# A decoder step on one core: other numbers for the planner of the recorded order, the two plain gate columns ahead of the two up columns, and the last residual block summed and squared in its bank

## The chip, the cores and the metric

One NeuronCore of a Trainium2 chip. The metric is the time of one execution on the device in microseconds, the median over the runs. The engines are TensorE (PE; its weight loads are shown apart as PEld), VectorE (DVE), ScalarE (ACT), GpSimd (POOL) and SyncE (SP), which issues most DMAs. Matmuls write to PSUM, eight banks of 128 x 512 fp32; everything else works in SBUF.

## The reference

One layer of a decoder for 512 prompt tokens and 8 x 4 sample tokens (544 columns in all), width 1024, fp32:

```
z = rmsnorm(x, norm_mix) @ w_in         # split: attention q, k, v; HGRN q, f, i, g
att = dilated_attention(q, k, v)        # 8 heads, three (window, dilation) patterns
f = lb + (1 - lb) * sigmoid(f);  o, s = hgrn2_recurrence(silu(q), 1 - f, i, log f)   # 4 heads
x = x + concat([head_rmsnorm(att), head_rmsnorm(o) * silu(g)]) @ w_out
x = x + cross_attention(rmsnorm(x, norm_cross), memory) @ w_co
u = rmsnorm(x, norm_ffn)
x = x + (silu(causal_conv3(u @ w_gate)) * (u @ w_up)) @ w_down      # 2816 columns
y = rmsnorm(x, norm_final)
```

The new keys and values, the HGRN states and the last gate rows are outputs too.

## The kernel before

All activations lie transposed in SBUF: x is eight tiles x[0] to x[7] of 128 features by 544 tokens. A product in fp32 accuracy is three fp32r matmuls (high by high, high by low, low by high part); weights are loaded (wr), cast to the high part by ACT (wh) and subtracted to the low part by DVE (wl). A token row is done in two cuts of 256 and 288 columns.

**The recorded order.** The kernel's code doesn't issue instructions. Every call goes to a `Tape` (line 240 on), which records it as a `Step` with its engine, length and dependences; at the end `run()` puts all steps in an order by a list scheduling on a model of the five engines, and issues them. All instructions so come from one line, L638 (DMAs L612). A product that is recorded under `main()` is a *main* step of PE; mains keep their recorded order. Other PE steps (scores, transposes, HGRN products) are *side* steps. When PE is free, the next main goes, unless side steps that are ready amount to `BURST` us, or the first of them has waited longer than `PATIENCE`, or one is due: then a burst of sides goes. A step's due time (`begin`) is reckoned back from its users (`due()`), with `MARGIN` us to spare ahead of a main; the other engines take steps up to `LEAD` us ahead of their due time, the earliest due first. The five numbers stand in line 259.

**The stages.** From 0 to about 320 us: the columns of w_in one after the other as mains (ps_z_q, ps_z_v and the like), among them as sides the dilated attention (psd, psS, psT, psO, psdo) and the four HGRN heads. A head's recurrence is done by levels: DVE makes the factors kq for windows of 1, 2, 4 and up to 64 tokens, PE multiplies them (psB for the smallest, psA, psL for the largest); ACT copies psA to hsm, POOL masks that to hvm, DVE adds up htm and hAT; psu, psU, hS carry the state; psin goes through DVE's hin and back through the same bank, and pso is the head's output. In the last head, memory products (ps_ck, ps_cv) are the mains. Then W_out, the cross-attention, and from 438 us the feed-forward.

**The feed-forward.** 22 column blocks of w_gate and w_up. The first `PLAIN` = 2 are plain products (`plain_tile`, line 2043; ps_g, ps_u in two cuts each). A gate column's bank is read out as ug by DVE (`weighed`), and goes through the convolution (ACT, then two DVE passes), silu (ACT) and a product with the row norm on DVE (cv); an up column's bank is read by the product with that (`up`). The other twenty go in pairs by a Strassen scheme of seven products (`Pair`; ps_ag, ps_dg, ps_cg and, for up, ps_au and so on), whose weight sums S1 to S4 and the part whg, wlg come from two weight columns; the sums S1g and S3g are made by a DMA that adds, issued by POOL. The first pair's first product (ps_ag with whg, wlg) stands ahead of the second half of the last plain column (`seq.insert(-1, ...)`, line 2270). The eight down blocks go in between, ps_d.

**The end.** The last four column blocks of w_down (`DOWN_LAST`) make eight blocks m in two cuts c, ps_dz, in three banks taken in turn (`PF`). For each, `last_half` (line 2317) adds the bank to x[m] (`add_to`, on DVE), squares the sum on ACT and adds that to ssq3's accumulator acc_final (on POOL, for m = 6 on DVE); for m = 7 the square stays apart as sq_last. `final(c)` (line 2336) sums over partitions by two matmuls (psr_final, on acc_final and on sq_last), makes 1/sqrt by Ln and two Exp on ACT (r_final in PSUM, r_fin in SBUF), multiplies into y and issues the output DMAs.

Of the kernel before, what the change touches and what calls it, by code (L numbers as in the profile page):

```python
# [250 lines left out]
class Tape:  # L251
# [4 lines left out]

    BURST, PATIENCE, SLACK, LEAD, MARGIN = 1.33, 3.05, 12.0, 12.06, 3.77


    BLOCK, FIRST, WAITS, FETCH = 256, 195, 1.0086, 6.0
# [380 lines left out]
def tile_decoder_step(ctx: ExitStack, tc: tile.TileContext, xT, memT, kwT, vw, s0, conv_in, mkT, mv, vecs, cst,  # L643
# [27 lines left out]
    def PF(name):  # L671

        turn[0] += 1
        return PDEC(name) if turn[0] % 3 == 0 else PD(name)
# [18 lines left out]
    def V(name, i=0):  # L693
        return vec[:, VEC_COLS[name][0] + i:VEC_COLS[name][0] + i + 1]
# [15 lines left out]
    resident |= {*range(len(specs), len(specs) + 12)}  # L710
    specs += [w_cq[i] for i in range(4)] + [w_co[i] for i in range(8)]
    ffn_w = len(specs)
    for j in range(PLAIN):
        specs += [w_gate[j], w_up[j]]

    class Weights:
        def __init__(self):
# [104 lines left out]
    stream = Stream()  # L822


    def passes(ps, w, xs, n0, n, order, first=True, last=True):
        for at, i in enumerate(order):
            (hi, lo), (xh, xl) = w[i], xs[i]
            for j, (a, b) in enumerate(((hi, xh), (hi, xl), (lo, xh))):
                nc.tensor.matmul(ps[:, :n], a, b[:, n0:n0 + n], start=(first and at == 0 and j == 0),
                                 stop=(last and at == len(order) - 1 and j == 2))  # L830

    def half(w, xs, name, evac, cut, order=None):
        n0, n = cut
# [1417 lines left out]

    gates, hids = {}, {}
    for q in range(2 * PLAIN):
        kind, j = "gu"[q % 2], q // 2
        done = plain_tile(kind, j, ffn_w + q, gates.get(j))
        if kind == "g":
            gates[j] = conv(j, done)
        else:
            hids[j] = gated(j, done)
# [46 lines left out]

    r_fin, last_sq = A("r_fin"), A("sq_last")
    hs, k = [hid[j] for j in range(*DOWN_LAST)], DOWN_LAST[1] - DOWN_LAST[0]
    ys = {}
    ON_POOL = (1, 3, 6), (1, 5)  # L2310

    def y_at(m, c):
# [4 lines left out]
    def last_half(m, c):  # L2317
        n0, n = LAST_CUTS[c]
        cut = slice(n0, n0 + n)
        if m == 0 and c == 1:  # L2320
            tape.gate_at = len(tape.mains) - 1
            nc.sync.dma_start(conv_out, last2)
            nc.scalar.preload_act_table_set(LN_SET)
            tape.gate_at = None
        ps = PF(f"ps_dz{m}_{c}")
        with tape.main():
            passes(ps, held[m], hs, n0, n, range(k))
        add_to(m)(ps, n0, n)
        if m < KT - 1:
            ssq3.add(x[m][:, cut], n0, nc.vector if m == KT - 2 else None)  # L2330
        else:
            nc.scalar.activation(last_sq[:, cut], x[m][:, cut], AF.Square)
        if m in ON_POOL[c]:
            nc.scalar.activation(y_at(m, c), x[m][:, cut], AF.Copy, scale=V("norm_final", m))

    def final(c):
        n0, n = LAST_CUTS[c]
        cut = slice(n0, n0 + n)
        ps = PX(f"psr_final{c}")
        for i, sq in enumerate((ssq3.acc, last_sq)):  # L2340
            nc.tensor.matmul(ps[:, :n], C("ones"), sq[:, cut], start=i == 0, stop=i == 1)
        nc.scalar.activation(r_fin[:, cut], ps[:, :n], AF.Ln, bias=eps, scale=1.0 / D)

        r = PX(f"r_final{c}")[:, :n]
        nc.scalar.activation(r, r_fin[:, cut], AF.Exp, scale=-0.5)
        nc.scalar.activation(r_fin[:, cut], r_fin[:, cut], AF.Exp, scale=-0.5)
        for m in range(KT):
            out = y_at(m, c)
            if m in ON_POOL[c]:
                nc.gpsimd.tensor_tensor(out, out, r_fin[:, cut], op=ALU.mult)  # L2350
            else:
                nc.vector.scalar_tensor_tensor(out, x[m][:, cut], V("norm_final", m), r, op0=ALU.mult, op1=ALU.mult)
            (nc.scalar if c and m % 2 else nc.sync).dma_start(yT[128 * m:128 * m + 128, cut], out)

    held = []
# [91 lines left out]
```

## Time and profile before

| | us |
|---|---|
| median of 3 runs | 820.3 (819.9, 820.3, 821.14) |
| the profiled run | 820.65 |
| its span | 818.8 |
| PE busy | 805.1 |
| DVE busy | 656.9 |
| ACT busy | 423.6 |
| POOL busy | 108.6 |

The span is from the first to the last event of the profiled execution; 1.85 us of its time lie outside. The granted clock of PE is 0.997 of full speed. A row of the timeline has the start, the length, the engine, the source line, the operation, out<-in by the program's names with buffer numbers left out, shapes, and in brackets how long the engine stood idle before it and what it waited for. A row of the waits of PE has what waited, for whom, the total, how often, and the longest.

### The profile page before, as it was taken

What the parts mean: (1) busy time and instruction counts of PE and PEld (TensorE: products, weight loads), DVE (VectorE), ACT (ScalarE), POOL (GpSimd) and SP (SyncE); (2) the same over time, 40 slices, a digit from 0 to 9 for tenths busy, and PEclk for the clock granted to TensorE, in tenths of its full rate; (3) what the DMA queues carried; (4) which work ended last, traced back from release to release, by engine and by line L of the source; (5) the groups of instructions that cost most, each with busy time, mean ns of one, the idle gap of its engine ahead of it and who ended that gap; (6) DMA issues with size and microseconds to landing.
All of it is one profiled execution on the core that took longest, in us unless ns stands there. A gap on an engine that the chain in (4) does not pass through costs nothing.

```text
span 818.8 us, 18897 instructions
## 1 busy us (share of the span) xinstructions
PE 805.1 (98%) x7515; PEld 755.4 (92%) x7515; DVE 656.9 (80%) x1486; ACT 423.6 (52%) x844; POOL 108.6 (13%) x187
## 2 busy tenths in 40 slices
PE   9999999999999999999999999999999999999996
PEld 9999986797889889998899999999999999999995
DVE  6997789987997997563679899987887788887854
ACT  7644364456557546444547655544554454445443
POOL 0040100010010000002201221222113012210113
PEclk9999999999999999999999999999999999999998
DMA  9439996956833544262522764556455565564503
GB/s 332 146 111 299 345 346 209 306 198 205 291 108 94 185 132 158 71 220 83 193 87 81 165 158 128 153 130 166 118 146 139 133 164 142 128 177 109 150 3 110
DMA packets 93064, 135.47 MB, mean 165 GB/s; under 512 B 6320, under 2 KB 60336, under 8 KB 92976
## 3 DMA queue, kind: packets, MB, share of 16 engines
q1 hardware_dynamic: 86208, 122.79, 46.5%
q0 software_dynamic: 5760, 10.49, 8.3%
q8 instruction: 59, 0.97, 0.5%
q10 hardware_dynamic: 1008, 0.99, 0.4%
q14 instruction: 29, 0.24, 0.1%
HBM read 126.17 MB, written 8.07 MB: 164 GB/s over the span
## 4 chain that ended last, share of the span: by engine, by line
PE 85%; DVE 9%; ACT 2%; DMA 2%; issue 1%; POOL 0%; SPq 0%; DVEq 0%
PE ps_d L638 13%; PE ps_ag L638 7%; PE ps_au L638 7%; PE ps_wo L638 6%; PE ps_cu L638 4%; PE ps_cg L638 4%; PE ps_co L638 3%; PE ps_dz L638 3%; PE ps_cq L638 3%; PE ps_z_v L638 2%; PE ps_du L638 2%; PE ps_dg L638 2%; DVE wl L638 2%; PE ps_z_Q L638 2%; PE ps_z_f L638 2%; PE ps_z_i L638 2%
## 5 line engine op out<-in xcount | busy, mean ns | idle before, releaser
L638 ACT CAST wh<-wr 128x1024 fp32r<-128x1024 f32 (+1 forms) x54 | 46.1, 871 | 57.0 <-issue 10.5
L638 DVE TENSOR_TENSOR wl<-wr,wh 128x1024 fp32r<-128x1024 f32 (+1 forms) x54 | 53.7, 1003 | 6.5 <-ACT wh L638 4.1
L638 DVE TENSOR_TENSOR xr<-xr,ps_d 128x256 f32<-128x256 f32 x80 | 34.7, 434 | 13.0 <-PE ps_d L638 12.6
L638 POOL COPY last<-ug 128x2 f32<-128x2 f32 (+1 forms) x44 | 22.1, 546 | 131.3 <-DVE ug L638 131.3
L638 DVE SCALAR_TENSOR_TENSOR cv<-ug,vec,cv 128x560 f32<-128x560 f32 x44 | 35.2, 800 | 1.0 <-ACT cv L638 0.2
L638 ACT ACTIVATE cv<-ug,vec 128x560 f32<-128x560 f32 x22 | 18.8, 857 | 27.9 <-DVE ug L638 27.9
L638 POOL TENSOR_TENSOR hvm<-hsm,cs 64x512 f32<-64x512 f32 x4 | 4.5, 1120 | 177.1 <-ACT hsm L638 132.6
L638 DVE TENSOR_TENSOR cv<-cv,r_ux 128x512 f32<-128x512 f32 (+1 forms) x44 | 18.9, 438 | 6.0 <-ACT cv L638 5.9
L612 POOL DMA_DIRECT2D S1u<-in_w_up x10 | 8.6, 861 | 100.4 <-DVE up L638 39.5
L638 POOL TENSOR_SCALAR cp<-cp,cden 128x256 f32<-128x256 f32 x8 | 7.9, 990 | 88.9 <-DVE cden L638 80.4
L638 ACT ACTIVATE P<-P,mx 128x128 f32<-128x128 f32 (+3 forms) x32 | 17.6, 552 | 3.7 <-DVE mx L638 3.7
L638 PE MATMUL ps_co<-coh,wh 128*128 128x256 f32 (+1 forms) x64 | 18.7, 292 | 0.0
L638 PE MATMUL ps_co<-coh,wl 128*128 128x256 f32 (+1 forms) x64 | 18.5, 289 | 0.0
L638 PE MATMUL ps_co<-col,wh 128*128 128x256 f32 (+1 forms) x64 | 18.4, 288 | 0.0
L638 ACT COPY keptg<-ps_ag 128x272 f32<-128x272 f32 x20 | 7.7, 383 | 20.1 <-PE ps_ag L638 20.1
L638 DVE TENSOR_TENSOR xr<-xr,ps_dz 128x288 f32<-128x288 f32 (+1 forms) x16 | 7.0, 438 | 13.3 <-PE ps_dz L638 13.3
L638 ACT COPY keptu<-ps_au 128x272 f32<-128x272 f32 x20 | 7.7, 385 | 19.1 <-PE ps_au L638 19.1
L638 DVE TENSOR_TENSOR keptg<-ps_cg,keptg 128x272 f32<-128x272 f32 x20 | 8.8, 440 | 10.8 <-PE ps_cg L638 10.4
L638 DVE TENSOR_TENSOR xr<-xr,ps_wo 128x256 f32<-128x256 f32 (+1 forms) x16 | 6.8, 437 | 12.5 <-PE ps_wo L638 12.5
L638 POOL COPY ug<-conv_state 128x16 f32<-128x16 f32 x22 | 14.8, 670 | 14.0 <-DMA conv_state<-in_conv_in 6.2
L638 DVE TENSOR_TENSOR keptu<-ps_cu,keptu 128x272 f32<-128x272 f32 x20 | 8.8, 438 | 9.7 <-PE ps_cu L638 9.7
L638 ACT ACTIVATE cv<-cv 128x560 f32<-128x560 f32 x22 | 14.8, 675 | 2.6 <-DVE cv L638 2.6
(3773 smaller groups left out, 3680.0 us busy)
## 6 DMA issues: line engine op xcount, KB each, us to landing
st<-in_kwT SPq DMA_DIRECT2D x32, 448.0 KB, 6.2
st<-in_vw SPq DMA_DIRECT2D x28, 512.0 KB, 6.1
wd<-in_w_down SPq DMA_DIRECT2D x32, 256.0 KB, 3.2
wr<-in_w_in SPq DMA_DIRECT2D x15, 512.0 KB, 6.9
wrg<-in_w_gate SPq DMA_DIRECT2D x10, 512.0 KB, 5.6
wru<-in_w_up SPq DMA_DIRECT2D x10, 512.0 KB, 5.5
st<-in_mkT SPq DMA_DIRECT2D x8, 512.0 KB, 4.8
wr<-in_w_out SPq DMA_DIRECT2D x8, 512.0 KB, 3.7
```

The lines of the kernel that those rows point to most:

```text
L612: return tape.put(engine, lambda: call(*args, **kw), outs, ins, 0.1, 0.3, size)
L638: return tape.put(engine, lambda: call(*args, **kw), outs, ins, length, lag, size, port, words)
```

## The change

It has three parts. The first sets other numbers in line 259 and so the order of the steps of the whole program. The second turns the order of the plain columns' weights and products from g0, u0, g1, u1 to g0, g1, u0, u1. The third concerns block m = 7 of the second cut: ACT copies x[7] into the bank ahead of the products, these accumulate on it without a start flag, ACT squares the bank directly, and the last product for y reads the bank, with the norm from SBUF (r_fin). The sum of the squares of m = 5 in this cut moves from POOL to DVE. The matmuls are the same in number and shape.

```diff
--- before.py
+++ after.py
@@ -256,7 +256,7 @@
 
 
 
-    BURST, PATIENCE, SLACK, LEAD, MARGIN = 1.33, 3.05, 12.0, 12.06, 3.77
+    BURST, PATIENCE, SLACK, LEAD, MARGIN = 0.77, 3.65, 12.0, 16.11, 3.44
 
 
     BLOCK, FIRST, WAITS, FETCH = 256, 195, 1.0086, 6.0
@@ -710,8 +710,7 @@
     resident |= {*range(len(specs), len(specs) + 12)}
     specs += [w_cq[i] for i in range(4)] + [w_co[i] for i in range(8)]
     ffn_w = len(specs)
-    for j in range(PLAIN):
-        specs += [w_gate[j], w_up[j]]
+    specs += [w_gate[j] for j in range(PLAIN)] + [w_up[j] for j in range(PLAIN)]
 
     class Weights:
         def __init__(self):
@@ -822,12 +821,12 @@
     stream = Stream()
 
 
-    def passes(ps, w, xs, n0, n, order, first=True, last=True):
+    def passes(ps, w, xs, n0, n, order, first=True, last=True, loose=False):
         for at, i in enumerate(order):
             (hi, lo), (xh, xl) = w[i], xs[i]
             for j, (a, b) in enumerate(((hi, xh), (hi, xl), (lo, xh))):
                 nc.tensor.matmul(ps[:, :n], a, b[:, n0:n0 + n], start=(first and at == 0 and j == 0),
-                                 stop=(last and at == len(order) - 1 and j == 2))
+                                 stop=(last and at == len(order) - 1 and j == 2), skip_group_check=loose)
 
     def half(w, xs, name, evac, cut, order=None):
         n0, n = cut
@@ -2251,7 +2250,7 @@
 
     gates, hids = {}, {}
     for q in range(2 * PLAIN):
-        kind, j = "gu"[q % 2], q // 2
+        kind, j = "gu"[q // PLAIN], q % PLAIN
         done = plain_tile(kind, j, ffn_w + q, gates.get(j))
         if kind == "g":
             gates[j] = conv(j, done)
@@ -2306,7 +2305,7 @@
 
     r_fin, last_sq = A("r_fin"), A("sq_last")
     hs, k = [hid[j] for j in range(*DOWN_LAST)], DOWN_LAST[1] - DOWN_LAST[0]
-    ys = {}
+    ys, last = {}, []
     ON_POOL = (1, 3, 6), (1, 5)
 
     def y_at(m, c):
@@ -2323,11 +2322,20 @@
             nc.scalar.preload_act_table_set(LN_SET)
             tape.gate_at = None
         ps = PF(f"ps_dz{m}_{c}")
+        whole = m == KT - 1 and c == 1
+        if whole:
+            tape.gate_at = len(tape.mains) - 1
+            nc.scalar.copy(ps[:, :n], x[m][:, cut])
+            tape.gate_at = None
         with tape.main():
-            passes(ps, held[m], hs, n0, n, range(k))
+            passes(ps, held[m], hs, n0, n, range(k), not whole, loose=whole)
+        if whole:
+            nc.scalar.activation(last_sq[:, cut], ps[:, :n], AF.Square)
+            last.append(ps[:, :n])
+            return
         add_to(m)(ps, n0, n)
         if m < KT - 1:
-            ssq3.add(x[m][:, cut], n0, nc.vector if m == KT - 2 else None)
+            ssq3.add(x[m][:, cut], n0, nc.vector if m >= KT - 2 - c else None)
         else:
             nc.scalar.activation(last_sq[:, cut], x[m][:, cut], AF.Square)
         if m in ON_POOL[c]:
@@ -2349,7 +2357,8 @@
             if m in ON_POOL[c]:
                 nc.gpsimd.tensor_tensor(out, out, r_fin[:, cut], op=ALU.mult)
             else:
-                nc.vector.scalar_tensor_tensor(out, x[m][:, cut], V("norm_final", m), r, op0=ALU.mult, op1=ALU.mult)
+                src, rows = (last[0], r_fin[:, cut]) if c and m == KT - 1 else (x[m][:, cut], r)
+                nc.vector.scalar_tensor_tensor(out, src, V("norm_final", m), rows, op0=ALU.mult, op1=ALU.mult)
             (nc.scalar if c and m % 2 else nc.sync).dma_start(yT[128 * m:128 * m + 128, cut], out)
 
     held = []
```

The order of the instructions changes most in the stages ahead of W_out. Two places there and one in the feed-forward:

PE in the first HGRN head (minus is before, plus is after; psd and psS are attention scores against the cache and the new keys, kq0_32 and kq0_64 the factors of the two largest windows, psA0 the middle windows):

```order
-L638 MATMUL psL0_196<-kq0_32_194 32x32 x8
+L638 MATMUL psS020_432<-z_k0_167,z_q0_223 128x384
+L638 MATMUL psS021_433<-z_k0_167,z_q0_223 128x384
+L638 MATMUL psd11_413<-st30_470,qbd_win_155 32x224 x4
 L638 MATMUL psA0_189<-kq0_8_188 32x32 x16
 L638 MATMUL psA0_189<-kq0_16_193 32x32 x16
 L638 MATMUL psA0_189<-cs_73,z_i0_175 32x128 x2
-L638 MATMUL psd11_413<-st29_469,qbd_win_155 32x224 x4
-L638 MATMUL psd11_413<-knew_156,qbd_win_155 32x32 x4
+L638 MATMUL psL0_196<-kq0_32_194 32x32 x8
 L638 MATMUL psL0_196<-kq0_64_197 64x64 x4
```

The scores psS02 come ahead of psA, and psL's first product goes behind psA.

PE in the last HGRN head (hsm, hin, hAT, hS are what DVE and ACT make of the products; ps_cv are the memory's value products):

```order
 L638 MATMUL psin3_806<-hst31_801,z_Q3_739 32x128 x4
+L638 MATMUL psu30_811<-hvm3_809,hsm3_794 128x512
+L638 MATMUL psu31_812<-hvm3_809,hsm3_794 128x512
+L638 MATMUL psin3_806<-hsm3_794 128x32
+L638 MATMUL psin3_806<-cs2_74,hin3_814 128x32 x2
+L638 MATMUL pso3_815<-hAT3_797,hvt3_807 128x128 x2
+L638 MATMUL pso3_815<-z_Q3_739,hS3_813 128x128
+L638 MATMUL pso3_815<-hAT3_797,hvt3_807 128x128
+L638 MATMUL pso3_815<-z_Q3_739,hS3_813 128x128
+L638 MATMUL pso3_815<-hAT3_797,hvt3_807 128x128
+L638 MATMUL pso3_815<-z_Q3_739,hS3_813 128x128
 L638 MATMUL ps_cv0_921<-wh19_924,mmh0_757 128x512
```

psu, psin's second use and pso now follow psin's first use at once; they stood among and behind the first six ps_cv products.

DVE in the plain columns, before (ug1 is the second gate column, S1g2 to S4g2 weight sums, wlg2 the low weight part of the first pair, cv1 the convolution):

```order
L638 TENSOR_TENSOR S1g2l_1263<-S1g2_1239,S1g2h_1262 128x512
L638 TENSOR_TENSOR h0l_1218<-up0_1214,h0h_1217 128x544
L638 TENSOR_TENSOR S2g2l_1242<-S2g2_1240,S2g2h_1241 128x512
L638 TENSOR_TENSOR S3g2l_1256<-S3g2_1254,S3g2h_1255 128x512
L638 TENSOR_TENSOR ug1_1221<-ps_g1_256_1223,r_ux_1129 128x256
L638 TENSOR_TENSOR ug1_1221<-ps_g1_256_1223,r_ux_1129 128x8x4
L638 TENSOR_TENSOR S4g2_1276<-S2g2_1240,wrg2_1230 128x512
L638 TENSOR_TENSOR wlg2_1232<-wrg2_1230,whg2_1231 128x1024
L638 SCALAR_TENSOR_TENSOR cv1_1224<-ug1_1221,vec_72,cv1_1224 128x560 x2
```

and after:

```order
L638 SCALAR_TENSOR_TENSOR cv1_1217<-ug1_1214,vec_72,cv1_1217 128x560 x2
L638 TENSOR_TENSOR up0_1220<-ps_u0_256_1222,cv0_1211 128x256
L638 TENSOR_TENSOR up0_1220<-ps_u0_256_1222,cv0_1211 128x32
L638 TENSOR_TENSOR S2g2_1240<-S1g2_1239,wrg2_1230 128x512
L638 TENSOR_TENSOR S3g2l_1256<-S3g2_1254,S3g2h_1255 128x512
L638 TENSOR_TENSOR wlg2_1232<-wrg2_1230,whg2_1231 128x1024
L638 TENSOR_TENSOR cv1_1217<-cv1_1217,r_ux_1129 128x512
L638 TENSOR_TENSOR up1_1228<-ps_u1_0_1229,cv1_1217 128x256
L638 TENSOR_TENSOR S2g2l_1242<-S2g2_1240,S2g2h_1241 128x512
```

wlg2 now follows S3g2l at once, and what concerned the second gate column is done before, save for cv1.

## The prediction

> **What bounds the kernel now.** I read the page first, then the waits of TensorE (PE), then the timeline at each of those waits, then sums by windows. The page:
>
> ```profile
> span 818.8 us, 18897 instructions
> PE 805.1 (98%) x7515; PEld 755.4 (92%) x7515; DVE 656.9 (80%) x1486; ACT 423.6 (52%) x844; POOL 108.6 (13%) x187
> ```
>
> PE works 805.1 of 818.8 us. The change leaves its matmuls as they are, so whatever it wins or loses is in the other 13.7 us, or in new waits. Where they lie, by the waits of PE (total, times, longest):
>
> ```profile
> PE psL L638 <- DVE kq L638: 1.5, 1, 1.5
> PE ps_g L638 <- DVE up L638: 1.3, 1, 1.3
> PE ps_first L638 <- DVE zero L638: 1.1, 1, 1.1
> PE psr_final L638 <- DVE acc_final L638: 0.8, 1, 0.8
> PE ps_z_q L638 <- DVE z_q L638: 0.5, 1, 0.5
> PE psA L638 <- DVE kq L638: 0.4, 1, 0.4
> PE psr_hg L638 <- DVE htm L638: 0.3, 1, 0.3
> PE ps_ag L638 <- DVE wlg L638: 0.2, 1, 0.2
> ```
>
> 6.1 us in eight waits; the rest, some 7.6 us, is nearly all the end, behind the last matmul. ps_first is the start and ps_z_q stands as it was; the other six lie in places that the new order rebuilds. That is the most there is to win by order, and a kernel so full can lose as easily: a wait that PE doesn't have today costs its whole length.
>
> **Part 1, the planner's numbers: head 1 of the HGRN part.** Here VectorE makes kq level by level and PE consumes it (psA, psL). Timeline rows (start, length, instruction):
>
> ```profile
> 121.37 0.56 PE L638 MATMUL psd<-st,qbd_win 128*32 128x224 f32 x8
> 121.48 0.42 DVE L638 TENSOR_TENSOR kq<-hq,hf 128x256 f32<-128x256 f32 x1
> 122.04 0.38 PE L638 MATMUL psL<-kq 128*32 128x32 f32 x13
> 123.27 0.26 ACT L638 COPY hsm<-psA 64x128 f32<-64x128 f32 x1 [0.17 <-PE psA L638]
> 123.61 1.14 POOL L638 TENSOR_TENSOR hvm<-hsm,cs 64x512 f32<-64x512 f32 x1 [18.88 <-ACT hsm L638]
> 123.77 1.26 DVE L638 TENSOR_TENSOR kq<-hq,hf 128x256 f32<-128x256 f32 x1
> 125.18 0.65 PE L638 MATMUL psL<-kq 128*64 128x64 f32 x8 [1.50 <-DVE kq L638]
> 129.29 0.92 PE L638 MATMUL psS<-z_k,z_q 64*128 64x384 f32 x4
> ```
>
> The last kq took 1.26 us where its like takes 0.42: it ran beside GpSimd's hvm. PE waited 1.50 for it. In the new order psS (0.9) and the psA products stand ahead of psL. PE got to this psL at 123.7 (125.18 less 1.50); with psS more and one psd and its companion less (0.5 by the first row) it gets there near 124.1. hsm and hvm move as well, by psS's 0.9 less the 0.35 of the smaller psL that stood ahead of psA and now stands behind it: hvm starts near 124.15. kq, on VectorE in its old place, starts at 123.77 and should end near 124.2. The 0.4 at psA goes too, with a psd product ahead of it. Gain 1.9 less a remainder of 0.1: **1.8** (0.6 if hvm is first again, 1.9 at best).
> On who is first, the Trainium skill says (SBUF — State Buffer, "SBUF: two separate sides") that VectorE with two SBUF inputs and GpSimd share a pair of ports as an exclusive lock, which whoever starts first keeps for its whole instruction. The row bears it out roughly: kq ended at 125.03, 0.28 after hvm. By it my 1.8 stands only while kq starts before hvm; by the rows alone I would have charged kq for the overlapped part and taken 1.5.
>
> The 0.3 at psr_hg, which now stands behind a whole product, goes (**0.3**); for new small waits in the same stretch, 135 to 205 us, I take **0.2** (0 to 0.7, the longest like it being psA's and psr_hg's together).
>
> **Part 1, heads 2 and 3.** There PE is full and VectorE nearly so. Windows: start and end, length, then busy time of PE, PEld, DVE, ACT, POOL. And the rows at both ends of the argument:
>
> ```profile
> 208.40:236.90 28.50, 28.50 (x465) 24.34 (x466) 27.52 (x75) 13.75 (x33) 1.03 (x1) 1.00 0.69 219
> 268.00:309.00 41.00, 40.78 (x522) 33.93 (x521) 39.80 (x88) 20.46 (x41) 2.01 (x2) 1.00 0.51 158
> 208.41 0.46 DVE L638 TENSOR_TENSOR z_i<-ps_z_i,r_mix 128x288 f32<-128x288 f32 x1 [1.27 <-PE ps_z_i L638]
> 217.46 0.45 DVE L638 TENSOR_TENSOR kq<-z_Q,z_f 128x272 f32<-128x272 f32 x1
> 223.50 0.47 PE L638 MATMUL psB<-kq 128*32 128x32 f32 x33
> 267.99 1.23 DVE L638 TENSOR_TENSOR wl<-wr,wh 128x1024 fp32r<-128x1024 f32 x1 [1.09 <-ACT wh L638]
> 298.95 0.42 DVE L638 TENSOR_TENSOR hin<-psin,cs 128x256 f32<-128x256 f32 x1
> 301.99 0.40 PE L638 MATMUL psin<-hsm 32*128 32x32 f32 x2
> ```
>
> VectorE works 27.5 of 28.5 us and 39.8 of 41.0. Today PE asks for its results late, with products of other stages between; the new order asks early. Head 2: the psB product on kq moves from 223.5 to about 216.7 (counting what stands ahead of it), while kq today ends at 217.9, 1.2 later; z_v, pushed behind two kq of 0.42 on VectorE, which overlap a little, would add up to 0.6, so the bounds are 0 and 1.8. Against it VectorE's 1.27 us hole before 208.41 is now filled with softmax work that stood later, which brings it that much ahead. I take **0.6**, for z_v. Head 3: psin and pso lose the ps_cv products that stood ahead of them; by counting along PE psin comes to about 295.9, but needs hin gone from its bank, which ends today at 299.4: 3.5 late. VectorE gets about 1.0 of this back by having hin ahead of two products that now stand behind it, and about 1.8 ahead of 267.99: the wait of 1.09 for ACT's cast goes, since ACT does its attention work earlier, and softmax work is done in the idle time before. That leaves **0.6** (0 to 2.7, the latter with only part of hin's move). The 0.2 us that PE is idle in the second window (41.00 less 40.78) I count as won.
>
> **Part 2, the plain columns.** Order g0, u0, g1, u1 becomes g0, g1, u0, u1.
>
> ```profile
> 454.16 0.69 DVE L638 TENSOR_TENSOR cv<-cv,r_ux 128x512 f32<-128x512 f32 x1 [0.76 <-ACT cv L638]
> 455.36 0.40 PE L638 MATMUL ps_g<-ux0h,wh 128*128 128x288 f32 x1 [1.32 <-DVE up L638]
> 458.55 0.62 ACT L638 CAST S3g2h<-S3g 128x512 fp32r<-128x512 f32 x1 [1.04 <-DMA S3g<-in_w_gate]
> 459.07 1.05 ACT L638 CAST whg<-wrg 128x1024 fp32r<-128x1024 f32 x1
> 460.84 1.22 DVE L638 TENSOR_TENSOR wlg<-wrg,whg 128x1024 fp32r<-128x1024 f32 x1
> 462.11 0.39 PE L638 MATMUL ps_ag<-ux0h,wlg 128*128 128x272 f32 x1 [0.19 <-DVE wlg L638]
> ```
>
> Today g1's second half waits 1.32 for a bank that u0's `up` frees only when g0's gate chain (silu's table, silu, cv) is through. With g1 ahead of u0 the banks are freed by plain copies of g, and the chain has two more products to run beside. But ps_ag then comes 1.5 us earlier and meets the next thing: S3g lands at 458.5 whatever PE does, ACT casts it and then whg (till 460.1), and VectorE's wlg can start at 460.15, not 460.84, ending near 461.4. ps_ag's first product with wlg so starts 0.7 earlier, not 1.5. Gain **0.7** (0 if wlg keeps its time, 1.5 if it doesn't matter).
>
> **Part 3, the last block.** The add of x[7] leaves the path: ACT copies x into the bank ahead, the matmuls accumulate on it, Square reads the bank.
>
> ```profile
> 807.28 0.42 ACT L638 ACTIVATE sq_final<-xr 128x256 f32<-128x256 f32 x1 [0.81 <-DVE xr L638]
> 809.37 0.28 PE L638 MATMUL ps_dz<-h21h,wdlz 128*128 128x256 f32 x1
> 809.68 0.42 DVE L638 TENSOR_TENSOR xr<-xr,ps_dz 128x256 f32<-128x256 f32 x1 [1.00 <-PE ps_dz L638]
> 810.02 0.42 DVE L638 TENSOR_TENSOR acc_final<-acc_final,sq_final 128x256 f32<-128x256 f32 x1
> 810.14 0.42 ACT L638 ACTIVATE sq_last<-xr 128x256 f32<-128x256 f32 x1 [1.00 <-DVE xr L638]
> 811.03 0.59 PE L638 MATMUL psr_final<-sq_last,cs 128*128 128x256 f32 x2
> ```
>
> Today: matmul, add (809.68), the sum of m=6 queued behind it on VectorE (810.02 to 810.44), psr_final on the sum, psr_final on sq_last at 811.03. After: both sums fit VectorE's idle 1.00 us before 809.68, so the first psr_final follows the last matmul; Square starts at 809.7, ends at 810.1, the second psr_final starts at 810.15. Gain **0.85** (0.5 if ACT reads the bank 0.35 slower, 0.9 at best). The ACT copy, 0.42 by its like, lies in ACT's idle 0.81 us before 807.28, ahead of the m=7 matmuls, which start near 808; without that hole it would delay them by 0.4. The y of m=7 multiplies by r_fin from SBUF, ready 0.4 after r_final; it stands second of six, so it waits at most 0.1.
>
> **Switches.** The chain of waits shows that twelve matmuls after a burst of side products take longer than twelve after their like:
>
> ```profile
> 58.74 1.70 PE ps_ck0k L638 x12
> 60.44 1.51 PE ps_ak0k L638 x12
> ```
>
> The new order alternates between the two kinds 46 times instead of 48: one burst less, **0.2** (0 to 0.4).
>
> **The sum.** Gains 1.8 + 0.3 + 0.2 + 0.7 + 0.85 + 0.2 = 4.05; losses 0.2 + 0.6 + 0.6 = 1.4; net 2.65. The profiled run took 820.65 us (818.8 and 1.85 around it), so 818.0; it stands 0.35 above the median of 820.3, so 817.6 for the median.
>
> **The rivals.**
> *All waits go:* heads 2 and 3 cost nothing, 4.05 and a little of the 0.8 more at ps_ag: 815.7. For it speaks that VectorE is not wholly full there; against, that psin's hin has 3.5 us to make up. 0.12.
> *Half of it:* head 1's collision comes back (1.2) or wlg keeps its time (0.7). If hvm starts before 123.77 on the new order's clock, kq ends 1.1 us late as today, and psL waits; the margin is 0.4 us. By the skill's rule above, this is decided by which of the two begins first. About 819.0, on the edge of what can be told. 0.13.
> *The heads eat it:* both at their upper bounds, 1.8 + 2.7 against 1.2: 3.3 worse than forecast, 820.9. 0.10.
> *Slower, hin:* VectorE keeps its present clock to hin, since it does 39.8 of 41.0 us there and nothing that PE wins ahead helps it. Then psin starts at 299.4 where its place is 295.9: 3.5 lost in head 3, all that was won ahead of it gone with it, and 1.65 won behind it (0.7, 0.85, 0.1): 822.1. It decides at a hin that ends after 297.5, in today's clock; I expect 295. For it: the full windows. Against: the hole before 208.41 and the ACT wait before 267.99, both of which end earlier in the new order. 0.10.
> The forecast has the remaining 0.55.
>
> **Range and chances.** A measurement can tell 0.2% here, 1.64 us: 818.66 and 821.94. Best case of all terms is 815.1, so 815.6 below; above, 820.9, which leaves out the slower rival and a few unknowns. Faster: 0.55 x 0.92, all of 0.12 and under half of 0.13: 0.67. Slower: 0.10 and a little of the heads: 0.11. The same: 0.22.
>
> **What would show it.** Right: in the waits of PE, psL, ps_g and psr_final are gone or under 0.3; ps_ag waits about 1.5; psin waits on hin and something of z_v shows, both under 1; kq beside hvm is 0.42; psr_final on sq_last starts 0.8 closer to the last ps_dz. Wrong: a wait over 1.5 us at psin or psB between 205 and 310 (heads), psL still over 1 (collision), or ps_ag over 2 (weights).

## The result and the profile after

The changed kernel takes 817.71 us (median of 6 runs, 816.75 to 818.72), the kernel before, run beside it on the same chip, 820.67 (6 runs). The ratio is 0.9963, with a 95% interval of 0.9950 to 0.9976: faster by 3.0 us. The forecast was 817.6 in a range of 815.6 to 820.9. The profiled execution took 817.74 us against 820.65 before, its span is 2.8 us shorter.

The first lines of its page:

```profile
span 816.0 us, 18919 instructions
PE 803.5 (98%) x7515; PEld 755.0 (93%) x7515; DVE 656.3 (80%) x1486; ACT 424.7 (52%) x845; POOL 108.3 (13%) x186
```

And the waits of PE in the changed kernel (what waited, for whom, total, times, longest):

```profile
PE ps_first L638 <- DVE zero L638: 1.1, 1, 1.1
PE psL L638 <- DVE mx L638: 0.8, 1, 0.8
PE ps_z_q L638 <- DVE z_q L638: 0.7, 1, 0.7
PE psU L638 <- ACT hkt L638: 0.6, 1, 0.6
PE ps_ag L638 <- DVE wlg L638: 0.6, 1, 0.6
PE psu L638 <- issue: 0.4, 1, 0.4
PE pst_hk L638 <- DVE hk L638: 0.3, 1, 0.3
PE psin L638 <- DVE hin L638: 0.3, 1, 0.3
PE ps_first L638 <- ACT wfh L638: 0.2, 1, 0.2
```

ps_g, psr_final, psA and psr_hg are gone from the list. psL is still there, but waits for something else (mx, not kq), and psU, psu, pst_hk and psin are new. The sum of the list is 5.0, it was 6.1; so over half of what was won is in no line of it. The first lines of the page say why: of the 2.8 us by which the span is shorter, 1.6 are busy time of PE (805.1 before, 803.5 now), for the same number of matmuls, and only 1.2 are idle time (13.7 before, 12.5 now). Where it was won shows better by place. The table gives, at the same product in each trace, how many microseconds later (+) or earlier (-) PE is there than in the profile of the kernel before. Each entry is a difference of two start times of one product (at the right end, of its end).

| kernel | 112 (start of w_in's i1) | 202 (i2) | 313 (W_out) | 438 (first gate column) | 464 (second up column, second cut) | 784 (ps_dz) | end of psr_final |
|---|---|---|---|---|---|---|---|
| changed | +0.42 | -0.89 | -0.33 | -0.22 | -1.52 | -1.99 | -2.80 |
| changed, second profile | +0.17 | -1.10 | -0.55 | -0.44 | -2.44 | -2.94 | -3.75 |
| tail alone | +0.02 | -0.15 | -0.24 | -0.24 | -0.30 | -0.29 | -1.10 |
| columns alone | +0.59 | +0.73 | +0.66 | +0.65 | -1.27 | -1.44 | -1.46 |
| numbers alone | -0.23 | -0.48 | +0.09 | +0.18 | -0.34 | -0.54 | -0.86 |

The first column is hardly the change: executions of one order differ there by several tenths (below). What counts is the step from one column to the next. In the first profile of the changed kernel the steps are -1.31, +0.56, +0.11, -1.30, -0.47 and -0.81.

**Head 1, 112 to 202.** (Head 1 is the first of the four, `h == 0` in the code; heads 2 and 3 are `h == 2` and `h == 3`. Behind the one between them, at 170 us, PE has no wait.) Timeline rows of the changed kernel:

```profile
124.31 0.42 DVE L638 TENSOR_TENSOR kq<-hq,hf 128x256 f32<-128x256 f32 x1
124.91 1.03 POOL L638 TENSOR_TENSOR hvm<-hsm,cs 64x512 f32<-64x512 f32 x1 [16.66 <-ACT hsm L638]
125.20 0.09 DVE L638 DVE_READ_ACCUMULATOR2_ANT mx<- 128x1 f32 x1
125.20 1.83 DVE L638 TENSOR_TENSOR wl<-wr,wh 128x1024 fp32r<-128x1024 f32 x1
125.34 1.05 PE L638 MATMUL psL<-kq 128*32 128x32 f32 x24 [0.81 <-DVE mx L638]
136.81 1.13 PE L638 MATMUL psu<-hvm,hsm 32*128 32x512 f32 x4 [0.44 <-issue]
```

kq takes 0.42, as its like, and is through before hvm begins. Now wl meets hvm and takes 1.83 instead of 1.21, but PE does not wait for that. It waits 0.81 at psL, although kq ended at 124.73.

**Heads 2 and 3, 202 to 313.** The new waits there, PE's rows, with those of what they wait for:

```profile
232.12 0.58 ACT L638 COPY hkt<-pst_hk 128x512 f32<-128x512 f32 x1
232.75 1.16 PE L638 MATMUL psU<-hvt,hkt 128*128 128x128 f32 x8 [0.65 <-ACT hkt L638]
285.21 1.03 POOL L638 TENSOR_TENSOR hvm<-hsm,cs 64x512 f32<-64x512 f32 x1 [41.94 <-ACT hsm L638]
285.31 1.22 DVE L638 TENSOR_TENSOR hG<-hG,z_f 128x256 f32<-128x256 f32 x1
288.38 0.71 DVE L638 TENSOR_TENSOR hk<-hk,hG 128x544 f32<-128x544 f32 x1
289.24 0.63 PE L638 MATMUL pst_hk<-cs,hk 128*128 128x128 f32 x4 [0.34 <-DVE hk L638]
295.01 0.42 DVE L638 TENSOR_TENSOR hin<-psin,cs 128x256 f32<-128x256 f32 x1
295.48 0.40 PE L638 MATMUL psin<-hsm 32*128 32x32 f32 x2 [0.27 <-DVE hin L638]
```

Head 2 pays at psU, where ACT's hkt is late, and not at z_v. Head 3 pays twice, 0.34 and 0.27. Ahead of both stands the collision of head 1 once more: hG, started 0.10 behind hvm, takes 1.22, where the hG before it took 0.41 (283.77), and from there to hin VectorE has no gap of more than 0.04. So what hG lost, 0.8, can reach hk and hin. In head 2 it is wl again that meets hvm (231.17, 2.06 instead of 1.21); hkt hangs on ACT there, not on wl.

**Plain columns, 438 to 464.** The rows between the gate chain and the first Strassen product:

```profile
448.75 1.17 POOL L612 DMA_DIRECT2D S3g<-in_w_gate  x1
457.71 0.62 ACT L638 CAST S3g2h<-S3g 128x512 fp32r<-128x512 f32 x1 [2.17 <-DMA S3g<-in_w_gate]
458.23 1.05 ACT L638 CAST whg<-wrg 128x1024 fp32r<-128x1024 f32 x1
459.31 1.23 DVE L638 TENSOR_TENSOR wlg<-wrg,whg 128x1024 fp32r<-128x1024 f32 x1 [0.26 <-ACT whg L638]
460.60 0.39 PE L638 MATMUL ps_ag<-ux0h,wlg 128*128 128x272 f32 x1 [0.58 <-DVE wlg L638]
```

The wait at ps_g is gone. ps_ag waits 0.58 for wlg, which starts at 459.31 (460.84 before). It hangs on ACT, which stood 2.17 us for S3g's landing, and S3g landed 0.84 earlier than before (457.71 against 458.55). POOL issued it 0.61 earlier (448.75 against 449.36); its own time was only 0.23 shorter.

**The end.** The rows behind the last block:

```profile
806.62 0.99 DVE L638 TENSOR_TENSOR acc_final<-acc_final,sq_final 128x256 f32<-128x256 f32 x2
807.37 0.28 PE L638 MATMUL ps_dz<-h21h,wdlz 128*128 128x256 f32 x1
807.67 0.70 PE L638 MATMUL psr_final<-acc_final,cs 128*128 128x256 f32 x2
807.69 0.39 ACT L638 ACTIVATE sq_last<-ps_dz 128x256 f32<-128x256 f32 x1 [0.53 <-PE ps_dz L638]
808.21 0.61 PE L638 MATMUL psr_final<-sq_last,cs 128*128 128x256 f32 x2
810.24 0.48 DVE L638 SCALAR_TENSOR_TENSOR y<-ps_dz,vec,r_fin 128x256 f32<-128x256 f32 x1
```

Both sums are through at 807.61, the first psr_final follows the last matmul, Square reads the bank 0.32 behind that matmul's start. psr_final on sq_last starts 0.84 behind the last matmul's start; before it was 1.66 (809.37 to 811.03).

### The profile page after: what moved, and what is told of

It reads as the page before. It is cut to its first block, busy times and chain, and to the rows that moved or that the text cites. A ratio compares the mean times of both kernels' runs of the same rounds, so it can differ in the third digit from the quotient of the medians.

```text
span 816.0 us, 18919 instructions
## 1 busy us (share of the span) xinstructions
PE 803.5 (98%) x7515; PEld 755.0 (93%) x7515; DVE 656.3 (80%) x1486; ACT 424.7 (52%) x845; POOL 108.3 (13%) x186
## 4 chain that ended last, share of the span: by engine, by line
PE 61%; DVE 4%; ACT 1%; DMA 1%; issue 0%; DVEq 0%
PE ps_d L638 13%; PE ps_ag L638 7%; PE ps_au L638 7%; PE ps_wo L638 6%; PE ps_cu L638 4%; PE ps_cg L638 4%; PE ps_co L638 3%; PE ps_dz L638 3%; PE ps_cq L638 3%; PE ps_dg L638 2%; PE ps_du L638 2%; PE ps_g L638 1%; DVE wl L638 1%; PE ps_cpo L638 1%; PE ps_cp L638 1%; PE ps_cv L638 1%
## 5 line engine op out<-in xcount | busy, mean ns | idle before, releaser
L638 DVE TENSOR_TENSOR xr<-xr,ps_d 128x256 f32<-128x256 f32 x80 | 34.7, 434 | 13.7 <-PE ps_d L638 12.9
L638 POOL COPY last<-ug 128x2 f32<-128x2 f32 (+1 forms) x44 | 19.9, 479 | 129.2 <-DVE ug L638 129.2
L638 DVE TENSOR_TENSOR cv<-cv,r_ux 128x512 f32<-128x512 f32 (+1 forms) x44 | 18.4, 436 | 3.4 <-ACT cv L638 3.0
L638 POOL COPY ug<-conv_state 128x16 f32<-128x16 f32 x22 | 18.4, 837 | 13.9 <-PE ps_co L638 5.8
L638 PE MATMUL ps_co<-col,wh 128*128 128x256 f32 (+1 forms) x64 | 18.4, 288 | 0.0
L638 PE MATMUL ps_co<-coh,wl 128*128 128x256 f32 (+1 forms) x64 | 18.4, 288 | 0.0
L638 DVE TENSOR_TENSOR xr<-xr,ps_wo 128x256 f32<-128x256 f32 (+1 forms) x16 | 6.8, 436 | 13.7 <-PE ps_wo L638 13.6
L638 PE MATMUL psdo<-st,dpt 128*32 128x256 f32 x224 | 16.3, 387 | 0.0
```

Source lines behind the costliest of these rows:

```text
L638: return tape.put(engine, lambda: call(*args, **kw), outs, ins, length, lag, size, port, words)
```

## The experiments

The theory after the result: the three parts add up, each at its own place; two of the waits that remain (psL, ps_ag) have causes that the prediction didn't name. The rivals: the planner's numbers carry most of the gain, or a part only pays in company of the others.

### The tail alone

The third part of the change put into the kernel before, as in the diff above, without the hunk of the numbers and the two of the columns.

> The kernel before with the tail's edit alone (the last block seeded with x by ScalarE, squared and scaled from the bank; one partial sum moved from GpSimd to VectorE). Theory A, the parts add up by their places: 0.8 us less, profiled about 819.85 us against 820.65, all of it behind the last matmul of the last block; the last Square reads ps_dz and stands 0.8 us nearer to that matmul; nothing ahead of 785 us moves by more than 0.15. Rival B, the tail's gain needs the new order ahead of it: under 0.4 us, 820.3 or more, with the copy of x or acc_final waited for.

Measured: 820.24 us median of 11 runs against 820.57 of the kernel before (33 runs, same chip); ratio 0.9995 (0.9986 to 1.0004). The profiled run took 819.94. By place, what the edit wins is behind the last block: -0.29 at 784, -1.10 at the end, 0.81 won there. The 0.29 is twice what was allowed for, but no more than executions of one order differ; and behind psr_final this execution took some 0.4 longer than the kernel before, so that its span is only 0.7 shorter. So it is theory A by place; the time by itself is too small to be told from none, and only the trace shows it.

### The columns alone

```diff
-    for j in range(PLAIN):
-        specs += [w_gate[j], w_up[j]]
+    specs += [w_gate[j] for j in range(PLAIN)] + [w_up[j] for j in range(PLAIN)]
...
-        kind, j = "gu"[q % 2], q // 2
+        kind, j = "gu"[q // PLAIN], q % PLAIN
```

> The kernel before with the new order of the four plain columns alone (two gates, then two ups). Theory A: 1.0 to 1.3 us less, 819.35 to 819.65 us profiled, all of it between 438 and 466 us; TensorE no longer waits at ps_g for a gate column's weights and waits 0.6 for wlg at the first Strassen product. Rival B, the order of the columns frees nothing by itself and the new planner numbers put wlg earlier: 0 to 0.3 us less, 820.35 or more, with the wait for wlg at the first Strassen product grown to the 1.5 that the ps_g wait loses.

Measured: 819.29 us (11 runs), ratio 0.9984 (0.9976 to 0.9993), profiled 819.43: theory A in time and place. Between 438 and 464 it won 1.92, more than expected, and PE waited for nothing there, not for wlg either, where 0.6 was foretold. That the profiled time still falls into the range of theory A is luck: this execution was 0.65 late at 438. The columns are the largest part of the change, and need none of the others.

### The numbers alone

```diff
-    BURST, PATIENCE, SLACK, LEAD, MARGIN = 1.33, 3.05, 12.0, 12.06, 3.77
+    BURST, PATIENCE, SLACK, LEAD, MARGIN = 0.77, 3.65, 12.0, 16.11, 3.44
```

> The kernel before with the planner's five numbers alone. Theory A: at 438 us it stands 0.2 us ahead of the kernel before (head 1 gains 1.3, heads 2 and 3 give 0.6 back, the start 0.4), and at the end 0.2 to 0.7 us ahead: 820.0 to 820.45 us profiled; psL waits for a bank (0.8, with mx named), psU for hkt, psin for hin, as in the changed kernel. Rival B, the numbers carry most of the gain: 1.5 us or more less, 819.1 or under, with wlg of the first Strassen product earlier than in the kernel before.

Measured: 819.88 us (11 runs), ratio 0.9993 (0.9984 to 1.0001), profiled 819.75. Not rival B. psL waits 0.8 for mx, psU 0.6 for hkt, psin 0.3 for hin, all as foretold. The profiled time is 0.25 below the range of theory A, though, and came about in other places than foretold. At 438 us it stands 0.18 behind the kernel before and not 0.2 ahead, for one row that the changed kernel does not have:

```profile
201.01 0.64 PE L638 MATMUL psdo<-st,dpt 128*32 128x256 f32 x8 [0.82 <-DMA st<-in_vw]
```

A load of cached values came 0.82 late here. Without that the step from 112 to 438 is -0.41, beside -0.64 and -0.61 in the two profiles of the changed kernel. From 438 to 464 it wins 0.52 with the old columns, where nothing was foretold: the wait at ps_g is there (1.35), that at ps_ag isn't. It also wins 0.32 behind 784, where psr_final now waits 0.2 for sq_last: the new order alone has part of what the tail's edit brings, so the two don't quite add up there.

### Columns and tail, with the old numbers

> The changed kernel with the old planner numbers: columns and tail alone. Theory A, the parts add up: 1.9 to 2.1 us less, 818.55 to 818.75 us profiled, that is, slower than the changed kernel by 0.7 to 1.0 and by the numbers' worth. Rival B, the numbers bring most: 819.8 or more. Third possibility, the numbers cost as much as they bring: 817.8, as the changed kernel.

Its edits are the two above together. Measured: 818.84 us (11 runs), ratio 0.9979 (0.9971 to 0.9988); profiled 819.43, of which 0.32 is a wait for wlg, 0.61 a late start at 438, and some 0.4 lies behind psr_final. The profiled time so misses theory A's 818.55 to 818.75, the median is 0.1 above it; rival B and the third possibility are each 1.0 away from the median. The three parts alone make -0.33, -1.28 and -0.69, -2.30 together; this one -1.73, where tail and columns alone make -1.61; the whole change -2.96 and -3.21 in its two measurements. Each difference of a part has an interval of some 0.7 us to either side, that of the whole 1.1, so the sum and the whole agree within what was measured; that the parts add up to better than 1 us is not shown by the medians.

### The changed kernel a second time

> The changed kernel a second time, beside the others on one chip: 817.7 us profiled. Theory A, TensorE's wait for wlg at the first Strassen product is set by when the DMAs S3g and wrg land (the three runs with the new column order showed 0, 0.3 and 0.6 us of it, with S3g cast at 457.20, 458.38 and 457.71 and TensorE 0.9, 0.8 and 0 us later than in the changed kernel at 438): it comes out somewhere between 0 and 0.8, and the span moves with it. Rival B, the wait belongs to the order with the new numbers: 0.6 again, whatever the landing. The wait at psL for mx comes out at 0.8 again by both, and no wait of 0.8 for a DMA at psdo if that of the run with the numbers alone was one execution's.

Measured: 817.30 us (6 runs), ratio 0.9966 (0.9953 to 0.9978), profiled 816.8, span 815.0. The order is the same, instruction for instruction, and the wait for wlg is not there. ACT's row for the cast, in this second profile:

```profile
456.35 0.62 ACT L638 CAST S3g2h<-S3g 128x512 fp32r<-128x512 f32 x1 [1.43 <-DMA S3g<-in_w_gate]
```

S3g landed 1.36 earlier than in the first profile (456.35 against 457.71), while PE was only 0.22 earlier at 438. The adding DMA is issued by POOL, 8.9 us ahead of the landing in the first profile of the changed kernel, 7.8 in the second. Over all runs with the new columns the time of this one DMA goes with PE's wait:

| kernel | S3g, issue to landing | PE's wait for wlg |
|---|---|---|
| changed, psL in a dense bank (below) | 9.3 | 0.74 |
| changed | 8.9 | 0.58 |
| columns and tail | 8.8 | 0.32 |
| changed, second profile | 7.8 | 0 |
| columns alone | 7.6 | 0 |

The same order comes out when the landing is counted from PE's start at 438: 20.1, 19.8, 19.6, 18.7 and 18.4. So theory A, with the landing of S3g as the cause. Nothing of 0.8 for a DMA at psdo either: that belonged to one execution.

### hvm on VectorE

The kernel before, with head 1's hvm taken from GpSimd:

```diff
-        nc.gpsimd.tensor_tensor(vm[:2 * NS], vs[:, None, :].to_broadcast([2 * NS, 4, 128]),
+        (nc.vector if h == 0 else nc.gpsimd).tensor_tensor(vm[:2 * NS], vs[:, None, :].to_broadcast([2 * NS, 4, 128]),
```

> The kernel before with head 1's hvm on VectorE, behind wl, in place of GpSimd (the heads after it unchanged). Theory A, the 1.26 us of kq are 0.42 of work and a wait for the port that hvm holds: kq comes out at 0.42, TensorE waits 0.6 to 0.8 at psL in place of 1.5, and the profile is 0.6 to 0.8 us shorter from there on, 819.85 to 820.05. Rival B, kq's length does not come from hvm: kq stays at 1.26, psL at 1.5, and VectorE's 0.7 more behind wl costs 0 to 0.5: 820.65 to 821.15.

Its rows where the kernel before had a kq of 1.26 and a wait of 1.50:

```profile
124.10 0.42 DVE L638 TENSOR_TENSOR kq<-hq,hf 128x256 f32<-128x256 f32 x1
124.44 1.22 DVE L638 TENSOR_TENSOR wl<-wr,wh 128x1024 fp32r<-128x1024 f32 x1
124.67 0.65 PE L638 MATMUL psL<-kq 128*64 128x64 f32 x8 [0.66 <-DVE kq L638]
126.04 0.67 DVE L638 TENSOR_TENSOR hvm<-hsm,cs 64x512 f32<-64x512 f32 x1
```

kq is back at 0.42 and PE waits 0.66: 0.84 won at this place, and the median is 819.41 (11 runs; ratio 0.9987, 0.9978 to 0.9996). Theory A: kq's 1.26 was 0.42 of work and a wait for hvm. By the medians, one instruction given to another engine was worth 1.1 us (0.3 to 1.8); by place it is 0.86 from 112 to 202, and another 0.48 came behind 438, where the edit does nothing (0.18 in the plain columns, 0.30 from 464 to 784). That is why the profiled 819.54 lies below the 819.85 to 820.05 foretold.

### psL in another bank

The changed kernel, with psL of head 1 in the pool of two dense banks. All engines keep their order.

```diff
-                bank["l"] = PX(f"psL{h}")
+                bank["l"] = (PX if h else PD)(f"psL{h}")
```

> The changed kernel with head 1's psL in one of the two dense banks in place of the five auxiliary ones; the order of every engine is unchanged. Theory A, TensorE's 0.8 us at psL wait for the bank that the four psS tiles now take ahead of it, until VectorE has read one: without that, psL starts when kq is done, 0.2 behind psA, and 0.6 us are gained, 817.1 to 817.2 profiled. Rival B, the bank is not what is waited for: 0.8 stays. Rival C, the dense bank is wanted by the z_v block behind it, which then waits for hAT's copies out of psL: TensorE waits 0.5 to 1.5 there, 817.5 to 818.5.

PE's rows there:

```profile
124.40 0.25 PE L638 MATMUL psL<-kq 128*32 128x32 f32 x2
124.48 0.29 PE L638 MATMUL psA<-cs,z_i 128*32 128x128 f32 x2
124.59 1.15 PE L638 MATMUL psL<-kq 128*32 128x32 f32 x22
125.67 0.39 PE L638 MATMUL ps_z_v<-xm0h,wh 128*128 128x256 f32 x1
```

psL begins without a wait and ps_z_v follows without one: theory A by place, rivals B and C fall, although the profiled 817.56 lies in rival C's range and above theory A's. The 0.8 was a wait for a bank. The five auxiliary banks hold psA and the four psS tiles, two of which the new order puts ahead of psL; VectorE has to read the first psS (its maximum is mx) before a bank comes free. In spite of that the median is 817.56 (5 runs; ratio 0.9964, 0.9951 to 0.9977), no less than the 817.30 of the changed kernel beside it. By place, 0.80 more is won from 112 to 202 (-2.07 against -1.27), and 0.74 is waited at ps_ag for wlg, with S3g 9.3 us on its way. In this execution the DMA took back what the bank gave.

### A partial sum alone

The kernel before with only the piece of the tail that takes block 5's sum from GpSimd to VectorE:

```diff
-            ssq3.add(x[m][:, cut], n0, nc.vector if m == KT - 2 else None)
+            ssq3.add(x[m][:, cut], n0, nc.vector if m >= KT - 2 - c else None)
```

> The kernel before with one piece of the tail's edit: block 5's partial sum on VectorE in place of GpSimd, nothing else. Theory A, the tail's 0.8 comes from the seeded bank, which takes VectorE's addition (0.42) and its hand-over off the last chain, and the sum alone only takes GpSimd's late addition away: 0 to 0.3 us less, 820.35 to 820.65 profiled, with psr_final's wait going from acc_final to sq_last. Rival B, GpSimd's late sum was the last to come and all of the 0.8: 819.85.

PE's rows at the end, of this kernel:

```profile
809.71 0.70 PE L638 MATMUL psr_final<-acc_final,cs 128*128 128x256 f32 x2
810.67 0.70 PE L638 MATMUL psr_final<-sq_last,cs 128*128 128x256 f32 x2 [0.26 <-ACT sq_last L638]
```

and of the one with the whole tail:

```profile
809.36 0.70 PE L638 MATMUL psr_final<-acc_final,cs 128*128 128x256 f32 x2
809.89 0.64 PE L638 MATMUL psr_final<-sq_last,cs 128*128 128x256 f32 x2
```

820.29 us (11 runs; ratio 0.9999, 0.9990 to 1.0008): no difference by time. The second psr_final follows the first by 0.96 here and by 0.53 with the seeded bank; by place the sum brings 0.32 from 784 to the end, the whole tail 0.81. Theory A at its upper end: the sum is worth 0.3, the seeded bank the other 0.5.

### The first pair's raw weights in a buffer of their own

```diff
-NBB = 18
+NBB = 16
...
-                self.raw = tape.tile(wgt, [128, 8, 128], F32, tag="wraw", name=f"wr{self.name}", bufs=3)
+                self.raw = (tape.tile(ffn, [128, 8, 128], F32, name=f"wr{self.name}") if (kind, j) == ("g", PLAIN)
+                            else tape.tile(wgt, [128, 8, 128], F32, tag="wraw", name=f"wr{self.name}", bufs=3))
```

> The changed kernel with a buffer of its own for the raw weights of the first Strassen gate pair (wrg), so that their load need not wait until VectorE has split the last plain column's weights; paid for with two of 18 FFN scratch tiles; the order of SyncE, ScalarE, VectorE and TensorE is unchanged. Theory A, wlg is late because wrg's load is issued only at 453.3 to 453.5 when a buffer comes free: now it is issued 2 to 3.5 us earlier, TensorE waits for wlg under 0.1, and from the longer of the two profiles of the changed kernel 0.6 are gained: 815.0 to 815.4 profiled span; the median 0.3 under the changed kernel's. Rival B, S3g's landing sets it, since ScalarE casts S3g2h ahead of whg: the wait for wlg stays between 0 and 0.7 with S3g's landing, and an earlier wrg makes S3g later, by up to the 1.3 us of a 512 KB load: 0.5 to 1.3 of wait, span 816 to 816.7.

The price is two of 18 scratch tiles (`NBB`). Measured, on another chip than the experiments so far: 816.76 us (5 runs), ratio 0.9954 (0.9940 to 0.9968), span 815.0. PE waits nowhere for wlg; nor did it in the second profile of the changed kernel, whose span is 815.0 too, so this one profile alone would not show what the buffer does. ACT's rows:

```profile
455.49 0.62 ACT L638 CAST S3g2h<-S3g 128x512 fp32r<-128x512 f32 x1 [0.46 <-DMA S3g<-in_w_gate]
456.59 1.05 ACT L638 CAST whg<-wrg 128x1024 fp32r<-128x1024 f32 x1 [0.47 <-PE ps_u L638]
```

The expectation had the outcome of theory A, but its reason was wrong. The load of wrg issued at 453.5 is the second pair's; the first pair's was issued at 432.6 and never late. SyncE's queue shows what the buffer does. The first and the last of five loads that stand together, in the changed kernel:

```profile
446.93 0.33 SPq L612 DMA_DIRECT2D wru<-in_w_up  x1
449.66 0.47 SPq L612 DMA_DIRECT2D A22g<-in_w_gate  x1
```

and with the buffer:

```profile
432.33 0.33 SPq L612 DMA_DIRECT2D wru<-in_w_up  x1
437.82 0.33 SPq L612 DMA_DIRECT2D A22g<-in_w_gate  x1
```

wru had to wait for the third shared buffer and held up the loads queued behind it; all of them then went out in the same 3 us as POOL's adding DMAs for S1g and S3g (447.98 and 448.75). With a buffer more they go 12 to 15 us earlier, and S3g takes 7.0 us in place of 8.9 (7.8 in the second profile); whg now waits for PE's ps_u (0.47) and no longer for S3g. Of rival B, that S3g's landing sets the wait is what the changed kernel showed; that the landing would come later falls: the second pair's wrg is indeed issued beside S3g now (446.68, 512 KB), but five loads left and two came, and S3g landed sooner. That the DMAs slow each other is read from this pair and from the table above; it was not measured by itself.

### The buffer and psL's bank together

> The same, and head 1's psL in a dense bank. Theory A: the 0.8 at psL and the wait for wlg are both gone, span 814.4 to 814.8 for a start as in the changed kernel, the median 0.9 to 1.2 under the changed kernel's 817.3 to 817.7. Rival B: the 0.8 gained at psL is waited again for S3g's landing behind ScalarE's cast: span 815.6 to 816.4.

Both edits above in the changed kernel. Measured: 816.12 us (5 runs, 815.75 to 816.87), ratio 0.9944 (0.9931 to 0.9956), span 814.5; S3g took 5.7 us, and neither psL nor ps_ag waits. Its median is the lowest of all, 1.2 to 1.6 us under the two of the changed kernel, which were not measured beside it; by theory A it should have been 0.9 to 1.2 under them. The intervals of the ratios still overlap a little (0.9956 here at the upper end, 0.9950 and 0.9953 there at the lower), so by time the gain over the changed kernel is likely and not settled. The bank, which won nothing by time alone, is worth 0.64 by the medians here (816.12 against 816.76 on one chip, 5 runs each), and 0.76 by place, from 112 to 202.

## Why the prediction was right, point by point

The sum was right (817.6 against 817.71), the terms less so. By place, forecast and first profile are: 112 to 202, -1.9 and -1.31; 202 to 313, +1.0 and +0.56; the plain columns, -0.7 and -1.30; 464 to 784, -0.2 at most (the switches) and -0.47; the end, -0.85 and -0.81; the start and the cross-attention, nothing and +0.53.

- **The frame.** "Whatever it wins or loses is in the other 13.7 us, or in new waits" did not hold. The idle time fell by 1.2 us and PE's busy time by 1.6, with the matmuls the same in number and shape; in the profiles of the parts it is 804.1 with the numbers, 804.7 with the tail and 805.1 with the columns. The sum of waits came out near the time all the same.
- **Head 1, 1.8 forecast, with 0.3 at psr_hg and 0.2 lost in small waits.** 1.9 net; measured 1.31 and 1.27. The named mechanism is right: kq ran before hvm and took 0.42, and the experiment with hvm on VectorE shows that hvm was the cause. On the Trainium skill's rule (SBUF — State Buffer, "SBUF: two separate sides"), that whoever starts first keeps the shared ports for its whole instruction, the trace agrees twice: kq started 0.60 ahead of hvm and was not held, and wl, started 0.29 behind hvm, ended 1.09 after hvm's end (125.94 to 127.03), nearly its own 1.21. The step that failed is "psS and the psA products stand ahead of psL", taken as a gain only: they stand ahead in the banks too, and psL waited 0.81 for one. That wait was not among the terms; another 0.44 at psu wasn't either.
- **Head 2, 0.6 forecast, for z_v.** The size is right (psU, 0.65), the place is not: z_v did not wait, ACT's hkt did the harm. A VectorE near its limit was read from the windows, and ACT, at 13.75 of 28.5 us, was not looked at; it was late in one instruction, with hAT, sq_mem and hsm queued ahead of hkt. That the size fits is luck, then.
- **Head 3, 0.6 forecast, at psin.** 0.27 there and 0.34 at pst_hk, 0.61 together. hin ended at 295.43, where the forecast said 295 and the rival 299.4. The slower rival so failed at its condition, a hin after 297.5. But the lateness is not that of a full VectorE alone: hG lost 0.8 beside hvm at 285.31, more than either wait. The prediction asked in head 1 who starts first and did not ask it in the heads behind. That both waits would go without this collision is read from VectorE's rows, not tried. From 202 to 313 the kernel lost 0.56, not 1.0: the stretch holds more gains than the 0.2 that was counted for small waits.
- **Plain columns, 0.7 forecast.** Measured 1.30 and 2.00 in the two profiles of the changed kernel, 1.92 alone. The failed step is "S3g lands at 458.5 whatever PE does". It landed at 457.7 and 456.35: in the first profile mostly because it was issued 0.61 earlier, in the second the DMA itself took 7.8 instead of 9.2 besides; this time spreads by more than the term. wlg began at 459.31 and not at 460.15, and in two of the five profiles with the new columns and the shared buffers PE did not wait for it at all. The upper bound of 1.5, the sum of the two old waits, was no bound either: the columns alone won 1.92.
- **The tail, 0.85 forecast.** 0.81, at every step as worked out: both sums in VectorE's idle time, Square 0.32 behind the matmul, no price for ACT reading PSUM, the copy of x hidden (ACT's 0.37 at 804.42).
- **Switches, 0.2.** Not told apart from the rest by any run.
- **Not in the forecast.** From 464 to 784 the changed kernel gains 0.47, in the second profile 0.50, with no wait in the list on either side. The tail alone gains nothing there, the columns alone 0.17, the numbers alone 0.20. It comes bit by bit up to about 700 us. What it is stays open.
- **The rivals.** "Half of it" (collision back, or wlg at its old time) and "the heads eat it" did not come; by its own terms (1.2, or 0.7) the first is 818.8 or 818.3, not 819.0. "All waits go" did not come either: the waits of heads 2 and 3 stand in both profiles, and the second one's time of 816.8 is 1.1 above its 815.7.
- **The signs.** ps_g, psr_final, kq's 0.42, psin's wait on hin and the 0.8 at the end came as named; psL at 0.81 was to be under 0.3, and z_v shows nothing. "ps_ag waits about 1.5" does not follow from the prediction's own numbers: PE comes 1.5 earlier and starts 0.7 earlier, which leaves a wait of 0.8. Measured were 0.58 and none.

So the total came right because errors cancelled: head 1 was given 0.6 too much and the heads behind it were charged 0.4 too much; the columns were given 0.6 too little, 0.3 to 0.5 came between 464 and 784 that nothing foretold, and against these stands a start that happened to be 0.4 later in this execution. That is luck as to the number. The second profile, 815.0 of span, shows the same kernel with a better landing of one DMA.

## What to carry to other kernels

When an order moves work ahead of a product, count banks and buffers as well as engines: a tile that goes ahead takes its bank along, and the next product waits for that as it would for data. A wait that stands at a DMA's landing is not a fixed time; look at what else is issued in the same microseconds; here, with those loads moved, two profiles showed no wait. A collision that an order removes in one place can come back in another: look at every instance of the two instructions, not only at the one that PE waits for today. And judge a change of a few tenths by its step between two places of the trace: the medians of 11 runs could not tell the tail's 0.8 from nothing, the two rows could.

## What the runs showed of the hardware

- One adding DMA of 256 KB, issued by GpSimd with the same requests around it, took 7.8 to 8.9 us in two executions of one kernel and 7.6 to 9.3 in the ten profiles in which the buffers are shared; 5.7 and 7.0 when five loads on SyncE's queue were gone from beside it and two had come.
- A VectorE TENSOR_TENSOR with both inputs in SBUF that started 0.10 to 0.29 behind GpSimd's hvm ended behind hvm by its own length less 0.12 to 0.14, in six cases: kq (123.77 and 169.42, kernel before) 0.28 of 0.42, htm (294.52, kernel before) 0.14 of 0.28, wl (125.20 and 231.17, changed kernel) 1.09 of 1.21, hG (285.31, changed kernel) 0.29 of 0.41. The other way round, hvm at 170.21 in the changed kernel began while VectorE was in an instruction of 0.48; VectorE's next htm took its usual 0.55, and hvm 2.37.
- The two old waits around the plain columns are 1.32 and 0.19, 1.51 together, and taking them away won 1.92 to 2.01. A wait so costs more than its length: with a partial sum alone the 0.19 at ps_ag isn't there, and PE is 0.32 earlier from ps_ag on, with the same order up to it. PE's busy time in that stretch says where the rest was: before, 209 matmuls in 26.49 us, 127 ns each; with the columns alone 224 in 28.00, 125 ns each. The quoted first products behind a wait take 0.39 or 0.40, their followers 0.28 to 0.30.

PE's windows from 438 to 466 us (start and end, length, busy time with count of PE, PEld, DVE, ACT and POOL, granted clock, DMA share, GB/s), of the kernel before:

```profile
438.00:466.00 28.00, 26.49 (x209) 26.07 (x209) 25.33 (x52) 16.76 (x28) 8.10 (x11) 1.00 0.47 115
```

and with the columns alone:

```profile
438.00:466.00 28.00, 28.00 (x224) 27.94 (x224) 26.23 (x54) 17.39 (x29) 5.26 (x10) 1.00 0.46 115
```

- Between executions with the same order up to there, PE's place at 112 us differs by up to 0.64 us with the old numbers (five profiles and that of the kernel before) and by 1.08 with the new (six profiles, -0.38 to +0.70 against the kernel before).
